# A hybrid convolution and RWKV-7 block: the last LayerNorm split between two phases, and a new fit of the clock that orders the trace

## The chip, the cores and the metric

The kernel runs on one core of one Trainium2 chip. The core has a matrix engine (TensorE, in the profile PE for matmuls and PEld for weight loads), a vector engine (DVE), a scalar engine (ACT), a general engine (POOL) and an engine that here only issues DMAs (SP). Each works through its own queue in order; semaphores join them. The metric is the device time of one execution in microseconds, the median of several runs.

## The reference

One decoder block with two token mixers over 2048 tokens of 1024 channels, all in float32:

```python
h = _rmsnorm(x, norm_g[l]) * (1.0 + scale[:, None, :]) + shift[:, None, :]
p = jnp.einsum('bsd,de->bse', h, w_in[l])
...
u = val * jax.nn.sigmoid(gate)
u = _causal_depthwise_conv(u, conv_k, conv_b)
u = _layernorm(u, ln_g, ln_b, LN_EPS)
u = jax.nn.silu(u) * jax.nn.silu(og)
y_conv = u @ w_o
...
o = _rwkv7_scan(r, decay, k, v, kk, kk * a)
o = _layernorm(o, gn_g, gn_b, GN_EPS)
o = (o + jnp.sum(r * k * r_k, axis=-1, keepdims=True) * v) * jax.nn.silu(og)
y_rwkv = o @ w_o
...
m = jax.nn.sigmoid(g_conv) * y_conv + jax.nn.sigmoid(g_rwkv) * y_rwkv
x = x + gate[:, None, :] * jnp.einsum('bsd,de->bse', m, w_out[l])
return _rmsnorm(x, final_g)
```

The LayerNorm of this study is the one over the 1024 channels of the convolution's output `u`, separately for each token.

## The kernel before

**Tiling.** The 2048 tokens are four blocks of TB = 512 (NB = 4). A tile is 128 channels by 512 tokens, so a block's convolution output is eight tiles (KT = 8). Each float32 matmul against a weight is three matmuls: the operand and the weight are each split into a rounded high part and the rest (`h_hi`, `h_lo`, `w_hi`, `w_lo`), and high-high, high-low and low-high are summed. One projection of 128 output channels is 8 x 3 = 24 matmuls of 512 columns.

**Two phases.** The first phase goes through the blocks b = 0 to 3. For each it projects 73 tiles of the input projection, runs the convolution's taps on DVE (`taps`: one multiplication and 30 multiply-adds a tile), and works the RWKV state in four groups g of four heads, in chunks of 64 tokens. Its results go to scratch in HBM: `z_d` (RWKV branch, gated), `y_d` (convolution output), `co_d` (its gate), `u_d` (convolution branch after LayerNorm and gates), `gr_d` and `gc_d`. At its end `rows0` does the two branch projections of block 0 ("ro" and "co"). The second phase does what is left, block by block: output projection with the residual (`pout`, `addx`), final RMSNorm (`tail_rs`, `finish`, store to `out`), and the branch projections of the next block (`rproj`, `cproj`). It loads z and u tiles (`lsplit`, through 8 load buffers `ld`) and splits them again. A finished x tile and the branch sum `mr` of the next block share one buffer, so `mr` waits for the store of `out`.

**The order of the first phase.** It is written out by a planner that runs while the kernel is traced. Tasks are Python generators with a rank; each `yield` gives a time from which the task may go on. `note` (line 89) keeps a model clock for each engine: an operation's time is a constant plus a slope times the elements per partition, by `RATE`, and for a DMA issue a constant on SP. PE's model time `now` moves with the projections, and between them `poll` lets each task go on whose time has come. So the modelled durations do not change an operation, but they set where it stands in its engine's queue, and so what a matmul behind it waits for. `Load.steps` also uses the clocks: the low part of a weight is made on POOL, or on DVE when POOL's clock is later than DVE's by more than 0.3 us (W2). Input weights are split in block 0 alone and kept in HBM (`kh_in`, `kl_in`). The second phase is ordered by the framework's own scheduler, from program order.

**Slots.** One slot is one group of one block: 6 projections for two pairs of heads (k, r, v each), and filler projections between them, given by FILL or, for the last block, by LAST ("c" is a convolution tile, "1" to "4" are gates). `order` puts FIRST fillers behind the first pair and the rest behind the second. `pair` makes the matrices of two heads (tiles KR, BK, As, tk, uv), `group` solves the triangular systems (a loop of POOL operations on `itmp` and `TT`, then small matmuls through `Tn` and `Qs`), runs the chain over 8 chunks (`S`, `Se`, `xo`), normalises and writes z. `slot` waits at its start until the group two before is normalised.

**Side work.** `sides` runs beside the slots: the next block's RMSNorm, the LayerNorm of the block before (`lnorm_first`), and `presplit`, which splits and stores weights of the second phase ahead of time. All draw their buffers from one ring `hx` of 7 tiles. The LayerNorm has three passes over the eight tiles: a sum (mean), centred squares with the centred tiles stored again (variance), and the last pass, which multiplies by the reciprocal root, applies the gain, bias, tanh and gate, and stores u. Each pass loads the tiles from HBM. For the last block `last_norm` runs all three, with its additions on DVE, once the last convolution tile is there; it has its own ring `more`, to which `lend(3)` gives three tiles of `hx`. The first operand of `rows0` (z of block 0) is loaded by `hload` from four items before the end of the last slot on.

Of the kernel before, what the change touches and what calls it, by code (L numbers as in the profile page):

```python
# [45 lines left out]
SLACK = 2.0  # L46
KEPT = ("in",)
# [4 lines left out]
FIRST = 5  # L52
AHEAD = 0.7
# [21 lines left out]
def hybrid_block(ctx: ExitStack, tc: tile.TileContext, x, vecs, convk, w2a2, final_g, ada, w_in, w_co, w_ro, w_o, crow, out,  # L75
# [12 lines left out]
    def note(name, op, out, ins):  # L88
        k_ = key(out)
        t = max([now[0], vt.get(name, 0.0), used.get(k_, 0.0) if name != "PE" or k_[:2] != "xo" else 0.0] + [ready.get(key(a), 0.0) + SEM for a in ins])  # L90
        if k_ not in ready and getattr(out.tensor, "tag", None):
            past, n = tags.setdefault(out.tensor.tag, []), out.tensor.tag_meta.bufs
            free_ = sorted((max(ready.get(q, 0.0), used.get(q, 0.0)) for q in past), reverse=True)
            if len(free_) >= n:
                t = max(t, free_[n - 1])
            past.append(k_)
            del past[:-3 * n]
        if name == "PE":
            if op == "transpose":
# [12 lines left out]
        elif name == "SP":  # L112
            vt["SP"] = t + 0.36
            vt["DMA"] = max(vt["DMA"], t) + size(out) * out.shape[0] * 4 / DMA_RATE
            end = vt["DMA"] + 1.9
        else:
            c0, c1_ = RATE[name] if op != "memset" else (0.1, 0.9e-3)
            end = vt[name] = t + c0 + c1_ * max([size(out)] + [size(a) for a in ins[:1]])
        ready[k_] = max(ready.get(k_, 0.0), end)
        for a in ins:  # L120
            used[key(a)] = max(used.get(key(a), 0.0), end)
# [154 lines left out]
    u_dram = scratch("u_d")  # L276

# [245 lines left out]
    hx = Ring(HXB, hx0)  # L523
    t2r = Ring(T2B, lambda name: e2.tile([P, TB], F32, name=name, tag="t2", bufs=T2B))
# [252 lines left out]
    def pair(G, q_, box):  # L777
        b, pr, uv, Asb = G.b, 2 * G.g + q_, G.uv, G.As[q_]
# [37 lines left out]
        yield ok(k)  # L816
        KR = l3.tile([P, NCH // 2, 4 * CH], F32, name="KR", tag="KR", bufs=KRB)
# [75 lines left out]
        yield when(lambda: "v" in box)  # L893
# [26 lines left out]
    def group(G, before):  # L920
        g, b, As, uv, R = G.g, G.b, G.As, G.uv, G.R
# [51 lines left out]
        yield when(lambda: G.pairs == 2 and (before is None or before.chained))  # L973
        yield ok(*As)
# [79 lines left out]
        locked[0] = False  # L1054
# [135 lines left out]
    convs = []  # L1190

    def taps(b, j, u, before):
# [18 lines left out]
    def lnorm_first(b, hx):  # L1211
# [9 lines left out]
        yield hx.room(3, 1)  # L1221
        ys, nxt = yload(0), yload(1)
        for j in range(1, KT):
            yj = nxt
            if j + 1 < KT:
                yield hx.room(1, 1)
                nxt = yload(j + 1)
            yield ok(ys, yj)
            eng.tensor_tensor(out=ys, in0=ys, in1=yj, op=ALU.add)
            hx.give(yj)  # L1230
# [34 lines left out]
        hx.give(qs, rt, mean)  # L1265
        def both_of(j):
            yj, ct = yload(j), hx.take("lnc")
            nc.sync.dma_start(ct, co_dram[b][j])
            return yj, ct

        nxt = None
        for j in range(KT):
            if nxt is None:
                yield hx.room(3, 1)
                nxt = both_of(j)
            else:
                yield hx.room(1)
            yj, ct = nxt
            th, nxt = hx.take("lnth"), None
            if j + 1 < KT and b + 1 == NB and hx.room(2)() is not None:  # L1280
                nxt = both_of(j + 1)
# [80 lines left out]
    def sides(b, g):  # L1362
# [51 lines left out]
    def order(b, g):  # L1414
# [31 lines left out]
    def slot(b, g, h, lora, new):  # L1446
        until(lambda: not Gs[:-1] or Gs[-2].normed)
# [129 lines left out]

    def cproj(b, uhl, mhl):
# [41 lines left out]
    for b in range(NB):  # L1620
# [73 lines left out]
        if b + 1 < NB:  # L1694
            uhl = lsplit(u_dram[b + 1], utiles())
# [40 lines left out]
```

## Time and profile before

| | |
|---|---|
| median of 3 runs | 2889.28 us |
| lowest and highest | 2885.52 and 2889.45 us |
| profiled execution, device time | 2893.26 us |
| its span, first to last instruction | 2891.5 us |
| granted TensorE clock, mean | 0.984 |
| ACT and POOL busy | 38% and 41% of the span |

The span is what the profile can explain; the device time of the same execution is 1.8 us longer. A group of instructions is named out<-in by the program's tiles. All first-phase instructions are recorded through one helper, so their line is that of the helper (L132) and the tile names tell them apart. A matmul's busy time includes part of its pipeline, so busy PE is not PE at its peak.

### The profile page before, as it was taken

Reading aid. Unit: us, or ns where it says so; the run is one execution under the profiler, and the core shown is the slowest. Engines: PE = TensorE matmul, PEld = TensorE weight load, DVE = VectorE, ACT = ScalarE, POOL = GpSimd, SP = SyncE. Lnnn points to the kernel's source line nnn. Section 1 sums busy time; section 2 is a strip of 40 time slices with the busy share of each in tenths; the row PEclk is TensorE's granted clock in tenths of the full one; section 3 lists DMA queues with packets and bytes.
Section 4 is the critical chain, followed back from the end, with each engine's and each line's share of the span. In section 5 each row is a group of like instructions: output and inputs, shape, how many; then the busy total and the mean of one; then the engine's idle time right before and its main releaser. Section 6 shows DMA issues by size and latency. Waiting matters only on the chain. (4 is left out here: it accounts for less than half of the span.)

```text
span 2891.5 us, 52406 instructions
## 1 busy us (share of the span) xinstructions
PE 2722.4 (94%) x19472; PEld 2195.2 (76%) x19472; DVE 2067.5 (72%) x3598; ACT 1092.9 (38%) x2181; POOL 1195.6 (41%) x1725
## 2 busy tenths in 40 slices
PE   6999999989999999999999998999999998999998
PEld 5777777767777777777777776877777777898988
DVE  6877887869677878886878786888887576343343
ACT  5545444434243434443434343324343334121211
POOL 1564746533528364534564553474543612000000
PEclk9999999989999999999999999999999999999999
DMA  8776867666758677767666776676665778777664
GB/s 329 258 286 206 292 218 265 236 233 228 235 185 290 199 255 242 275 222 238 231 251 223 249 255 197 220 269 215 227 230 191 273 247 315 259 239 247 215 226 175
DMA packets 370959, 697.26 MB, mean 241 GB/s; under 512 B 135184, under 2 KB 153936, under 8 KB 370704
## 3 DMA queue, kind: packets, MB, share of 16 engines
q1 hardware_dynamic: 370704, 693.91, 70.3%
q8 instruction: 154, 2.52, 0.4%
q14 instruction: 101, 0.83, 0.1%
HBM read 500.63 MB, written 192.02 MB: 240 GB/s over the span
## 5 line engine op out<-in xcount | busy, mean ns | idle before, releaser
L132 PE MATMUL ps_main<-h_hi,w_hi 128*128 128x512 f32 x2432 | 1016.3, 418 | 16.7 <-DVE lora L132 4.6
L132 PE MATMUL ps_main<-h_hi,w_lo 128*128 128x512 f32 x2432 | 966.9, 398 | 25.3 <-POOL w_lo L132 14.6
L132 PE MATMUL ps_main<-h_lo,w_hi 128*128 128x512 f32 x2432 | 961.3, 395 | 0.5 <-DVE h_lo L132 0.5
L132 DVE SCALAR_TENSOR_TENSOR acc<-u,ck,acc 128x512 f32<-128x512 f32 x928 | 698.0, 752 | 27.9 <-POOL u L132 2.2
L132 PEld LDWEIGHTS ps_main<-h_hi,w_lo 128*128 128x128 f32 x2432 | 462.2, 190 | 140.1 <-POOL w_lo L132 18.7
L132 PEld LDWEIGHTS ps_main<-h_hi,w_hi 128*128 128x128 f32 x2432 | 463.3, 190 | 128.4 <-issue 13.3
L132 PEld LDWEIGHTS ps_main<-h_lo,w_hi 128*128 128x128 f32 x2432 | 463.7, 191 | 96.3 <-issue 8.7
L132 POOL TENSOR_TENSOR w_lo<-w_st,w_hi 128x1024 fp32r<-128x1024 f32 (+1 forms) x82 | 165.0, 2012 | 332.5 <-ACT w_hi L132 288.5
L132 ACT ACTIVATE th<-ps_main 128x512 f32<-128x512 f32 x160 | 95.5, 597 | 360.2 <-PE ps_main L132 311.5
L132 POOL TENSOR_TENSOR TT<-TT,itmp 128x126 f32<-128x126 f32 (+22 forms) x496 | 209.5, 422 | 38.9
L132 POOL TENSOR_TENSOR itmp<-La,TT 128x126 f32<-128x126 f32 (+22 forms) x496 | 203.5, 410 | 37.7 <-issue 7.9
L132 ACT CAST w_hi<-w_st 128x1024 fp32r<-128x1024 f32 (+1 forms) x135 | 127.4, 945 | 221.6 <-DMA w_st<-w_co_t 78.4
L132 DVE SCALAR_TENSOR_TENSOR S<-xo,pe,Se 64x64 f32<-64x64 f32 x512 | 145.0, 283 | 91.9 <-PE xo L132 69.4
L132 ACT COPY uv<-xo 64x256 f32<-64x256 f32 (+1 forms) x192 | 81.2, 439 | 251.3 <-PE xo L132 184.7
L132 DVE TENSOR_TENSOR w_lo<-w_st,w_hi 128x1024 fp32r<-128x1024 f32 x53 | 74.5, 1405 | 68.3 <-PE ps_main L132 51.6
L132 DVE TENSOR_TENSOR As<-aux,maskA 128x512 f32<-128x512 f32 x128 | 82.3, 685 | 49.0 <-PE aux L132 48.9
L132 ACT ACTIVATE Se<-S,pe 128x128 f32<-128x128 f32 x256 | 89.0, 397 | 67.2 <-DVE S L132 66.7
L132 PEld LDWEIGHTS aux<-KR,BK 64*128 64x128 f32 x1024 | 66.3, 191 | 44.3 <-POOL KR L132 21.1
L132 PE MATMUL aux<-KR,BK 64*128 64x128 f32 x1024 | 80.0, 290 | 20.7 <-POOL KR L132 14.0
L132 POOL TENSOR_TENSOR wlo<-wf,wl 64x128 fp32r<-64x128 f32 x64 | 31.3, 489 | 159.2 <-ACT wl L132 156.7
L132 DVE TENSOR_TENSOR xt<-pout,xt 128x256 f32<-128x256 f32 x64 | 24.4, 420 | 100.1 <-PE pout L132 100.1
L132 PEld LDWEIGHTS xo<-S,KR 128*128 128x128 f32 x512 | 77.1, 189 | 20.7 <-ACT Se L132 4.3
(283 smaller groups left out, 5005.4 us busy)
## 6 DMA issues: line engine op xcount, KB each, us to landing
w_hi<-kh_in SPq DMA_DIRECT2D x219, 512.0 KB
w_lo<-kl_in SPq DMA_DIRECT2D x219, 512.0 KB
w_st<-w_in_t SPq DMA_DIRECT2D x73, 512.0 KB
kh_in<-w_hi SPq DMA_DIRECT2D x71, 512.0 KB
kl_in<-w_lo SPq DMA_DIRECT2D x71, 512.0 KB
lny<-y_d SPq DMA_DIRECT2D x96, 256.0 KB
w_hi<-kh_ro SPq DMA_DIRECT2D x32, 512.0 KB
w_lo<-kl_ro SPq DMA_DIRECT2D x32, 512.0 KB
```

What stands on the lines that cost most here:

```text
L132: r = f(*a, **k)
```

## The change

**The last LayerNorm.** For the last block, `taps` copies the first finished convolution tile to a sum tile and adds each later one to it. `lnorm_first` then starts with the sum that is given to it and leaves out the first pass. After the reciprocal roots it stores them (`rl_d`) and ends; the last pass of the last block is done by `ulast` in the second phase, ahead of the last `cproj`, from `y_d`, `co_d` and `rl_d`, and its result is split at once, without going through `u_d`. For the other blocks the last pass keeps its form, without a branch for loading the next pair of tiles early, which only the last block took. `lend` gives one tile, not three.

**The clock.** A DMA issue takes 0.45 us of SP's clock, not 0.36; an ACT operation takes 0.1 us more for each operand beyond the first; the scan's slope is doubled; a DVE multiply-add of 64 elements takes 0.08 us more.

**The slots.** A slot no longer waits for the group two before. Instead `pair` allocates its As tile once that group's chain has ended, and the uv tile is allocated when that group is normalised; `group` loads its matrices (`La`) once the group before has merged its own. In the last slot one filler stands behind the first pair instead of five (FIRST_LAST), and the loads of z start 9 items before the end instead of 4 (HLAST). The 16 pre-splits are spread over blocks 1 to 3 as 1, 1, 2, 2 and 1, 1, 2, 2 and 1, 1, 1, 1 a slot (LATE_W), instead of 1, 1, 3, 3 in blocks 1 and 2.

```diff
+LEND = 1
+LATE_W = ((), (1, 1, 2, 2), (1, 1, 2, 2), (1, 1, 1, 1))
+FIRST_LAST = 1
+HLAST = 9
...
         elif name == "SP":
-            vt["SP"] = t + 0.36
+            vt["SP"] = t + 0.45
...
             c0, c1_ = RATE[name] if op != "memset" else (0.1, 0.9e-3)
-            end = vt[name] = t + c0 + c1_ * max([size(out)] + [size(a) for a in ins[:1]])
+            n_ = max([size(out)] + [size(a) for a in ins[:1]])
+            if name == "ACT":
+                c0 += 0.1 * max(len(ins) - 1, 0)
+            elif op == "tensor_tensor_scan":
+                c1_ *= 2
+            elif name == "DVE" and op == "scalar_tensor_tensor" and n_ == CH:
+                c0 += 0.08
+            end = vt[name] = t + c0 + c1_ * n_
...
     def pair(G, q_, box):
...
+        yield when(lambda: G.prior is None or G.prior.chained)
+        Asb = l3.tile([P, 2, NCH, P], F32, name="As", tag="As", bufs=ASB)
+        G.As.append(Asb)
...
-        yield when(lambda: "v" in box)
+        yield when(lambda: "v" in box and (G.prior is None or G.prior.normed))
+        if q_ == 0:
+            G.uv = l3.tile([P, NCH, 2, P], F32, name="uv", tag="uv", bufs=2)
...
     def opened(b, g, h, lora):
...
-        G.uv = l3.tile([P, NCH, 2, P], F32, name="uv", tag="uv", bufs=2)
+        G.merged = False
+        G.prior, G.uv, G.As = Gs[-2] if len(Gs) > 1 else None, None, []
-        G.As = [l3.tile([P, 2, NCH, P], F32, name="As", tag="As", bufs=ASB) for _ in range(2)]
...
     def group(G, before):
...
+        yield when(lambda: before is None or before.merged)
         La = lt.tile([P, 32, 32], F32, name="La", tag="La", bufs=1)
...
     def taps(b, j, u, before):
...
+        if b + 1 == NB and j == 0:
+            yield hx.room(1)
+            ysum.append(hx.take("ysum"))
+            nc.scalar.copy(ysum[0], yj)
+        elif b + 1 == NB:
+            yield ok(ysum[0], yj)
+            nc.vector.tensor_tensor(out=ysum[0], in0=ysum[0], in1=yj, op=ALU.add)
...
-    def lnorm_first(b, hx):
+    def lnorm_first(b, hx, ys=None):
...
+        if b + 1 == NB:
+            yield ok(rl)
+            nc.sync.dma_start(rl_d, rl)
+            hx.give(rl)
+            return
...
     def sides(b, g):
...
-                yield from lend(3)
+                yield from lend(LEND)
         if b:
-            for _ in range(0 if b + 1 == NB else (1, 1, 3, 3)[g]):
+            for _ in range(LATE_W[b][g]):
...
-        yield from lnorm_first(NB - 1, more)
+        yield from lnorm_first(NB - 1, more, ysum[0])
...
-            yield from fill(FIRST if q == 0 else len(todo))
+            yield from fill(len(todo) if q else FIRST_LAST if (b, g) == (NB - 1, 3) else FIRST)
...
     def slot(b, g, h, lora, new):
-        until(lambda: not Gs[:-1] or Gs[-2].normed)
...
-            if new is not None and rest == 4:
+            if new is not None and rest == (4 if b + 1 < NB else HLAST):
...
+    def ulast(hl):
+        rl = f2.tile([P, TB], F32, name="rl", tag="rl", bufs=1)
+        nc.sync.dma_start(rl, rl_d)
+        for j in range(KT):
+            yt, ct = ldt("yt", y_dram[NB - 1][j]), ldt("ct", co_dram[NB - 1][j])
+            th = ob.tile([P, TB], F32, name="uth", tag="uth")
+            nc.vector.tensor_tensor(out=yt, in0=yt, in1=rl, op=ALU.mult)
+            nc.scalar.activation(th, yt, AF.Tanh, scale=hlg[:, j:j + 1], bias=hlb[:, j:j + 1])
+            nc.scalar.activation(yt, yt, AF.Identity, scale=vc("conv_ln_g", j), bias=vc("conv_ln_b", j))
+            nc.vector.scalar_tensor_tensor(out=yt, in0=th, scalar=1.0, in1=yt, op0=ALU.add, op1=ALU.mult)
+            nc.vector.tensor_tensor(out=yt, in0=yt, in1=ct, op=ALU.mult)
+            split(hl[0][j], hl[1][j], yt, nc.vector)
+        return hl
...
-            uhl = lsplit(u_dram[b + 1], utiles())
+            uhl = lsplit(u_dram[b + 1], utiles()) if b + 2 < NB else ulast(utiles())
```

More of the change, by code (lines that the diff above doesn't have):

```diff
@@ L276, in hybrid_block @@
     u_dram = scratch("u_d")
+    rl_d = dp.tile([P, TB], F32, name="rl_d", tag="rl_d")
     grow_d = dp.tile([D], F32, name="grow_d", tag="grow_d")
@@ L523, in hybrid_block @@
     hx = Ring(HXB, hx0)
+    hx1 = hx
     t2r = Ring(T2B, lambda name: e2.tile([P, TB], F32, name=name, tag="t2", bufs=T2B))
@@ L777, in pair @@
     def pair(G, q_, box):
-        b, pr, uv, Asb = G.b, 2 * G.g + q_, G.uv, G.As[q_]
+        b, pr = G.b, 2 * G.g + q_
         wf = e1.tile([P, 2, P], F32, name="wf", tag="wf")
@@ L892, in pair @@
         nc.scalar.copy(rk, pb)
-        yield when(lambda: "v" in box)
+        yield when(lambda: "v" in box and (G.prior is None or G.prior.normed))
+        if q_ == 0:
+            G.uv = l3.tile([P, NCH, 2, P], F32, name="uv", tag="uv", bufs=2)
+        uv = G.uv
         vv = box["v"]
@@ L920, in group @@
     def group(G, before):
-        g, b, As, uv, R = G.g, G.b, G.As, G.uv, G.R
+        g, b, As, R = G.g, G.b, G.As, G.R
         yield when(lambda: G.tri == 2)
@@ L973, in group @@
         yield when(lambda: G.pairs == 2 and (before is None or before.chained))
+        uv = G.uv
         yield ok(*As)
@@ L1053, in group @@
                     cp(As[q][prow(e), :, e::2, rcol(e)], pg[e].rearrange("p c (h n) -> p h c n", h=2)[prow(e ^ q)])
-        locked[0] = False
+        locked[0], G.merged = False, True
         O = uv[:, 0::2]
@@ L1188, in conv @@
         evac(value(project(h, ("in", T_VAL + j)), convs[-3:-2]))
-    convs = []
+    convs, ysum = [], []
     def taps(b, j, u, before):
@@ L1220, in lnorm_first @@
         eng = nc.vector if b + 1 == NB else nc.gpsimd
[L1221 to L1230, printed above, removed]
+        if ys is None:
+            yield hx.room(3, 1)
+            ys, nxt = yload(0), yload(1)
+            for j in range(1, KT):
+                yj = nxt
+                if j + 1 < KT:
+                    yield hx.room(1, 1)
+                    nxt = yload(j + 1)
+                yield ok(ys, yj)
+                eng.tensor_tensor(out=ys, in0=ys, in1=yj, op=ALU.add)
+                hx.give(yj)
         yield burst(ok(ys), free, bank("late"))
@@ L1264, in lnorm_first @@
                 yield idle("DVE", 0.3)
-        hx.give(qs, rt, mean)
-        def both_of(j):
-            yj, ct = yload(j), hx.take("lnc")
-            nc.sync.dma_start(ct, co_dram[b][j])
[L1269 to L1281, printed above, removed]
+        hx.give(qs, rt)
+        hx1.give(mean)
+        if b + 1 == NB:
[4 more added lines that the diff above has]
+        for j in range(KT):
+            yield hx.room(3, 1)
+            yj, ct, th = yload(j), hx.take("lnc"), hx.take("lnth")
+            nc.sync.dma_start(ct, co_dram[b][j])
             yield ok(yj, rl)
@@ L1576, in lsplit @@
         return hi, lo
+    def ulast(hl):
+        rl = f2.tile([P, TB], F32, name="rl", tag="rl", bufs=1)
+        nc.sync.dma_start(rl, rl_d)
+        for j in range(KT):
+            yt, ct = ldt("yt", y_dram[NB - 1][j]), ldt("ct", co_dram[NB - 1][j])
[7 more added lines that the diff above has]
+        return hl
     def cproj(b, uhl, mhl):
```

## The prediction

> **What bounds the kernel now.** I read the page first: the span, the busy shares and the slices.
>
> ```profile
> span 2891.5 us, 52406 instructions
> PE 2722.4 (94%) x19472; PEld 2195.2 (76%) x19472; DVE 2067.5 (72%) x3598; ACT 1092.9 (38%) x2181; POOL 1195.6 (41%) x1725
> ...
> PE   6999999989999999999999998999999998999998
> ...
> DVE  6877887869677878886878786888887576343343
> ```
>
> TensorE is the bound. It is busy for 2722 of 2891.5 us, its work is the same matmuls after the change, and so a change can only win the 169 us in which it stands idle, and what a lowered clock adds to them. VectorE is next: seven to eight tenths through the first phase, three to four tenths in the last fifth. So I asked second where the idle time lies, stage by stage (columns: stretch, length, busy time and count of PE, PEld, DVE, ACT, POOL, granted clock, DMA share, GB/s).
>
> ```profile
> core 0: us, PE busy (x) PEld busy (x) DVE busy (x) ACT busy (x) POOL busy (x), PEclk, DMA share, GB/s
> ...
> 2300.00:2310.00 10.00, 6.98 (x25) 5.13 (x24) 3.79 (x6) 4.26 (x7) 8.04 (x19) 0.84 0.88 341
> ...
> 2360.00:2410.00 50.00, 44.86 (x244) 35.75 (x243) 46.35 (x70) 24.52 (x39) 22.58 (x10) 1.00 0.64 212
> ...
> 2420.00:2440.00 20.00, 12.63 (x99) 11.55 (x98) 12.43 (x22) 10.86 (x24) 0.00 (x0) 0.91 1.02 373
> ...
> 2702.00:2748.00 46.00, 46.00 (x389) 45.84 (x388) 12.61 (x27) 11.99 (x38) 0.00 (x0) 1.00 0.57 202
> ...
> 570.00:600.00 30.00, 19.43 (x63) 14.28 (x63) 25.53 (x34) 5.81 (x9) 25.73 (x53) 0.78 0.85 314
> ```
>
> The reader is to see three kinds of stretch. From 2300 to 2440, where the first phase hands over to the second, PE idles 3.0, 5.1 and 7.4 us in the three quoted pieces. In the second phase (2702 to 2748) it is never idle, and DVE has 33 of 46 us free. In the first phase there are stretches such as 570 to 600, with 10.6 us idle. A lowered clock comes with the worst of them: 0.78 of 30 us is 6.6 us more, 0.84 of 10 us is 1.6, 0.91 of 20 us is 1.8.
>
> Third, the chain of waits over the handover.
>
> ```profile
> 2398.93 4.60 DVE lny L132 x2
> ...
> 2405.12 1.04 ACT w_hi L132
> 2406.24 2.67 POOL w_lo L132
> ...
> 2420.74 5.32 DMA zt<-z_d
> 2426.07 6.92 DMA xt<-x_in
> 2433.05 7.24 DMA w_lo<-kl_o
> ```
>
> Here the last pass of the last LayerNorm (tile lny) stands directly ahead of a weight split that PE needs, and then three loads follow one another: the second phase's first tiles are fetched only when the first phase lets go, and the weights of the output projection queue behind them.
>
> **The last pass, moved.** Part by part, beginning with what leaves the first phase.
>
> ```profile
> L132 DVE SCALAR_TENSOR_TENSOR lny<-lnth,lny 128x512 f32<-128x512 f32 x8 | 9.4, 1173 | 0.6 <-ACT lny L132 0.4
> ...
> L132 DVE TENSOR_TENSOR lny<-lny,lnr 128x512 f32<-128x512 f32 x7 | 8.1, 1153 | 0.1
> L132 DVE TENSOR_TENSOR lny<-lny,lnc 128x512 f32<-128x512 f32 x8 | 7.6, 954 | 0.0
> ...
> L132 ACT ACTIVATE lnth<-lny,hlb,hlg 128x512 f32<-128x512 f32 x8 | 6.5, 811 | 9.7 <-DVE lny L132 9.7
> ```
>
> These rows are of 2343 to 2416 alone. Three DVE operations for each of 8 tiles, 25 us, and two ACT operations of about 0.81 us each, 13 us, leave the stretch in which DVE is at 46.35 of 50 us. With them go 24 transfers (y and conv gate in, u out), and one small store of the reciprocal roots comes in. PE's 5.1 us of idle in 2360 to 2410 is not all theirs: the group chain and the load of the next operand tiles stay. I take half, **-2.6 us**; ends 0 and -5.1.
>
> In the second phase the same operations come back as ulast, with two loads per tile instead of one. There POOL does nothing, and the nearest row, the split of the same tile, gives the price of one two-input operation.
>
> ```profile
> L132 DVE TENSOR_TENSOR u_lo<-zt,u_hi 128x512 fp32r<-128x512 f32 x24 | 15.3, 687 | 7.4 <-ACT u_hi L132 7.4
> ```
>
> 24 operations of 0.69 us are 16.5 us of DVE, and 16 of 0.81 us are 13.0 us of ACT. They lie beside the third block's output projection, whose 46 us (2702 to 2748) have 33.4 us of DVE and 34.0 us of ACT free: hidden. One tile worked alone is 4 DVE and 3 ACT operations, 4 x 0.69 + 2 x 0.81 + 0.6, about 5 us; eight in strict sequence would be 40 us, still inside. If that cover failed, what waits is the end of the block, which has no slack:
>
> ```profile
> 2753.53 4.11 DMA out<-xt
> ...
> 2757.77 0.70 DVE mr L132
> 2758.51 76.46 PE ps_main L132 x336
> ```
>
> PE starts on the result of `mr` at once, and `mr` needs a tile freed by the output store. Every microsecond by which ulast keeps DVE past 2748 is paid. Behind ulast's loads, which wait for one of 8 load buffers, SyncE's queue holds the weight loads of the next projections; they are loaded two pairs ahead, more than one tile's 5 us. I put **+1.5 us**, ends -0.5 and +6.
>
> **The sum, moved.** The first pass was 7 DVE additions and 8 loads after the last convolution tile. Now it is one ACT copy and the same 7 additions, each behind its tile, and no loads. Work on DVE is unchanged, and the mean is there as soon as the eighth tile is. Second pass and roots stay. Cost nothing: the additions ride with the taps, which have the lowest rank, and the last convolution (c7) stands in the third of the last block's four groups; without that cover it would be 7 x 0.9 = 6 us of DVE at the handover. The price is the row of the additions:
>
> ```profile
> L132 DVE TENSOR_TENSOR lny<-lny 128x512 f32<-128x512 f32 x15 | 12.8, 856 | 11.7 <-DMA lny<-y_d 11.6
> ```
>
> **The last group and the operand loads.** HLAST starts the loads of the first phase-two operand 9 items before the end, no longer 4. Between 2300 and 2440 the waits of PE say who lacked them:
>
> ```profile
> PE ps_main L132 <- ACT h_hi L132: 2.8, 1, 2.8
> ```
>
> This is the 3.0 us idle of 2300 to 2310, and the 1.6 us of clock with it: **-4.4 us**; ends 0 and -4.6. [...] The quoted stretch shows 0.84 with a longest wait of 2.8 us, so the measurement decides and the clock stays in.
>
> FIRST_LAST puts the last pair of heads behind one filler projection, not five. Its triangular solve and its chain now end inside the tail:
>
> ```profile
> L132 POOL TENSOR_TENSOR itmp<-La,TT x31: 239/410/892, 2273.6 to 2308.6; 128x126 f32<-128x126 f32 x3, 128x30 f32<-128x30 f32 x2, 128x56 f32<-128x56 f32 x2, 128x78 f32<-128x78 f32 x2
> ...
> L132 DVE STREAM_TRANSPOSE Tn<-As x8: 392/433/443, 2323.0 to 2329.4; 32x256 f32<-32x256 f32 x8
> ```
>
> Four projections less ahead of it are at least 22 us (24 matmuls each, at 76.46 / 336 = 0.23 us by the chain row above), so the chain starts near 2300 or before, and the stretch after 2380 holds little but projections. Together with the vanished last pass, whose tiles hold space up to the end of its stretch, 2416, the 8 x loads and 8 z loads can go out before the last projection ends instead of at 2420, and the weights behind them come sooner. What PE loses there is 7.4 us idle and 1.8 us of clock. I take two thirds, **-6.1 us**; ends 0 (the operand tiles of the last projection hold the space, not the LayerNorm) and -9.2.
>
> **The order of the first phase.** The clock that orders the trace now charges 0.45 us for a DMA issue, 0.1 us per extra ACT operand, a doubled slope for the scan (0.15 + 512 x 0.0022 = 1.28 us, from 0.71) and 0.08 us more for the state update (0.30 from 0.22). It changes no operation, only where each stands in its queue. The rows that it was held against:
>
> ```profile
> L132 DVE SCALAR_TENSOR_TENSOR S<-xo,pe,Se 64x64 f32<-64x64 f32 x512 | 145.0, 283 | 91.9 <-PE xo L132 69.4 <-ACT Se L132 5.7 <-issue 1.8
> ...
> L132 DVE TENSOR_TENSOR_SCAN M<-keep,M 128x512 f32<-128x512 f32 x32 | 44.4, 1388 | 8.4 <-ACT M L132 8.1
> ```
>
> ```profile
> 2420.26 1.37 SPq L132 DMA_DIRECT2D zt<-z_d  x3
> ```
>
> 283 ns, 1388 ns, and 1.37 / 3 = 0.46 us for an issue: each new charge is nearer than the old one. So matmuls are placed later where they used to be placed ahead of their inputs. What that can win are PE's waits between 60 and 2295 us for ACT and DVE:
>
> ```profile
> PE aux L132 <- ACT sq L132: 12.9, 13, 3.2
> PE ps_main L132 <- POOL w_lo L132: 12.8, 6, 4.6
> PE late L132 <- DVE Tn L132: 11.3, 7, 3.3
> PE aux L132 <- DVE As L132: 6.3, 8, 2.7
> ...
> PE aux L132 <- ACT tk L132: 4.0, 10, 1.5
> PE xo L132 <- DVE uv L132: 3.7, 7, 1.0
> ```
>
> Without the POOL row they are 38.2 us. One operation's charge is only part of what makes an input late, and a new order makes waits of its own, so I take a quarter, **-10 us**; ends -38 (all of them) and +17 (one more stretch like 570 to 600, 10.6 idle and 6.6 of clock). The other waits that the change adds (for the earlier group's chain, normalisation or merge, in place of one wait for all at the start of a slot) hold back the placing of instructions, no engine; I count them here, with the four weight pre-splits that move from blocks 1 and 2 into block 3, whose results are first read after 2440.
>
> **Sum.** -2.6 + 1.5 - 4.4 - 6.1 - 10 = -21.6 us against the profiled execution's 2893.3 us, or 2871.7. That execution is 4.0 us above the median of the runs shown, 2889.3; from there it is **2868 us**.
>
> **Rivals.** *The tail has another wall.* If space for the second phase is let go by the last projection itself, the handover stays: -15.5 us, 2874. For it: the x loads follow the end of the last projection at once. Against: w_lo comes last of all, behind 16 loads that need not wait for it. 12 in 100. *The fit does more.* If half of the 38.2 us goes and half of 570 to 600's loss with it, the order term is -28, and with the whole handover, 9.2, the time is 2847. 14 in 100. *No change.* The order term turns to +11, as waits of new places replace those of old ones, and the tail's gain is spent: 2889. 12 in 100. *Slower, by the choice of engine for the weight splits.* The planner gives a split to DVE when POOL's clock is more than 0.3 us behind.
>
> ```profile
> L132 POOL TENSOR_TENSOR w_lo<-w_st,w_hi 128x1024 fp32r<-128x1024 f32 (+1 forms) x82 | 165.0, 2012 | 332.5 <-ACT w_hi L132 288.5
> ...
> L132 DVE TENSOR_TENSOR w_lo<-w_st,w_hi 128x1024 fp32r<-128x1024 f32 x53 | 74.5, 1405 | 68.3 <-PE ps_main L132 51.6
> ```
>
> The new fit makes DVE's clock later, by 2 x 0.57 + 32 x 0.08 = 3.7 us a group, and leaves POOL's, so more splits go to POOL, at 2.0 us instead of 1.4. In block 0, where each input tile is split once, POOL is busy 25.73 of 30 us in 570 to 600, and PE waits there for w_lo. A second stretch of that kind, 17.2 us, and the other half of the 12.8 us doubled, 6.5, make +23.7 in place of -10: 2889.3 - 11.6 + 23.7 = 2901. It decides from the point where the order term passes +17.4. Against: DVE at 25.53 of 30 us there has no more room than POOL. 15 in 100.
>
> **Chances.** My forecast 47, and with it the other wall 12 and the stronger fit 14: faster 73 in 100; no change 12; slower 15. A difference of 0.2%, 5.8 us, is about what a measurement of this kernel can tell from none. The range 2846 to 2894 leaves out half of the stronger fit and some two thirds of the slower case.
>
> **What would show it.** Right: PE's wait for h_hi near 2300 is gone; no lny operation after about 2340, and u's operations on DVE between two output stages late in the run with PE still busy throughout; the idle time at the handover under 4 us; PE's waits for sq and Tn smaller. Wrong: a PE gap where the fourth block starts (ulast not hidden), waits for POOL's w_lo above 13 us in the first block, or a handover that still idles 7 us.

## The result, and the profile after

The changed kernel takes **2863.03 us** (median of 4 runs, 2856.74 to 2867.68), the kernel before 2887.60 us beside it (4 runs): a ratio of 0.9909, interval 0.9887 to 0.9931. The profiled execution took 2867.68 us, its span 2866.0 us, against 2893.26 and 2891.5 us: 25.6 us less. The median lies 5 us under the forecast of 2868 us and inside its range. Several of the forecast's terms were nevertheless far off, and their errors cancel, as the experiments show.

The page of the changed kernel, the lines that stand for those shown of before (the span, PE's busy time, and PE and DVE in 40 slices):

```profile
span 2866.0 us, 52384 instructions
PE 2712.4 (95%) x19472; PEld 2198.5 (77%) x19472; DVE 2056.0 (72%) x3596; ACT 1091.8 (38%) x2182; POOL 1194.2 (42%) x1727
...
PE   6999999989899999999999999999999998998998
...
DVE  6877787868677787886778787898887564335343
```

PE runs the same 19472 matmuls. So the 25.5 us of span are idle time, or the lengthening that goes with it. To see where, I cut both traces at places with the same work behind them. The table by stretches, first of the kernel before, then of the changed one (columns as in the prediction):

```profile
60.00:2300.00 2240.00, 2128.29 (x15755) 1678.44 (x15754) 1746.21 (x2991) 911.95 (x1810) 1155.29 (x1682) 0.99 0.70 238
...
60.00:2428.00 2368.00, 2245.01 (x16670) 1772.01 (x16669) 1845.20 (x3150) 961.36 (x1894) 1192.01 (x1715) 0.99 0.71 239
2428.00:2880.00 452.00, 439.43 (x2629) 391.82 (x2628) 170.47 (x308) 96.68 (x219) 0.00 (x0) 0.99 0.70 240
```

```profile
60.00:2270.00 2210.00, 2117.62 (x15770) 1681.14 (x15768) 1738.96 (x2990) 909.46 (x1808) 1148.79 (x1693) 0.99 0.71 239
...
60.00:2391.00 2331.00, 2230.83 (x16670) 1771.89 (x16669) 1817.72 (x3122) 947.91 (x1878) 1190.60 (x1717) 0.99 0.71 239
2391.00:2860.00 469.00, 444.31 (x2637) 395.92 (x2635) 191.91 (x362) 109.69 (x239) 0.00 (x0) 0.97 0.69 238
```

The first 15,755 matmuls took 2240 us, and 15,770 now take 2210: **30 us** less. The whole first phase and the handover, 16,670 matmuls each time, went from 2368 to 2331 us: **37 us**, of which the tail of the first phase has 7. The second phase gave some back: from these cuts to the end of the span it is 463.5 us before and 475.0 us now. That is **+12 us**, and the idle time in the rows doubled from 12.6 to 24.7 us. The three make -25. Of the first 37, 23 are idle time (123.0 to 100.2 us). The other 14 are busy time of the same number of matmuls. The records of matmuls overlap (those of pout at 2690 us in the changed kernel start 0.12 us apart and last 0.28 us each). The sum of busy time fell with no matmul less, and what the 14 us are made of stays open.

What the first phase's waits became (waits of PE between 60 and 2295 us in the changed kernel; total us, times, longest):

```profile
PE aux L143 <- POOL KR L143: 20.4, 11, 6.7
PE ps_main L143 <- POOL w_lo L143: 12.9, 7, 3.3
PE late L143 <- DVE Tn L143: 8.1, 6, 2.5
...
PE aux L143 <- ACT tk L143: 6.1, 10, 1.5
...
PE aux L143 <- ACT sq L143: 3.4, 7, 0.8
...
PE aux L143 <- DVE As L143: 2.2, 3, 0.9
...
PE xo L143 <- DVE uv L143: 1.3, 4, 0.4
```

The waits for sq, Tn, As and uv that the prediction had named fell from 34.2 to 15.0 us; tk, which it had named too, rose from 4.0 to 6.1, and w_lo stayed. One is new in size, KR with 6.7 us at its longest. Its cause stands in the trace of POOL, row by row (start, duration, then in brackets the idle time before it and what ended it):

```profile
775.99 1.26 POOL L143 TENSOR_TENSOR w_lo<-w_st,w_hi 128x512 fp32r<-128x512 f32 x1 [5.61 <-ACT w_hi L143]
777.21 1.17 POOL L143 TENSOR_TENSOR KR<-r,E 128x512 f32<-128x512 f32 x1
```

Half of a weight split (128x512 is the shape of the pre-splits, which aren't needed before the second phase) stands in front of KR in POOL's queue and waits 5.6 us for w_hi, and PE waits for the KR behind it.

The handover still idles. The chain of waits there, and the stretch's row:

```profile
2377.92 5.28 PE ps_main L143 x23
2383.20 0.10 SPq L143
...
2383.87 6.59 DMA zt<-z_d
```

```profile
2383.00:2403.00 20.00, 12.34 (x99) 11.33 (x97) 12.94 (x22) 9.50 (x22) 0.00 (x0) 0.93 1.00 358
```

Idle are 7.7 us of 20, against 7.4 before. The first of the loads goes out within 0.2 us of the end of the last projection (2383.20), and the last thing that the last LayerNorm does is to store its roots, some 80 us sooner:

```profile
L143 SPq DMA_DIRECT2D rl_d<-lnr x1: 319/319/319, 2300.8 to 2300.8; - x1
```

So it isn't the LayerNorm that held their space.

In the second phase the loss is one gap. The stretch at the start of the third block:

```profile
2578.00:2602.00 24.00, 14.04 (x55) 10.99 (x55) 21.55 (x46) 10.80 (x18) 0.00 (x0) 0.79 0.95 346
```

PE is idle for 10.0 of 24 us, at a clock of 0.79. Something of ulast is in the way there, though ulast is written behind the *third* block's output projection. DVE started it a block early, at the end of the *second* (operations on ulast's tile yt: count, shortest, median and longest ns, first and last start):

```profile
L143 DVE TENSOR_TENSOR yt<-yt,rl x8: 684/691/693, 2577.4 to 2611.6; 128x512 f32<-128x512 f32 x8
```

What it does there is seen on DVE's own rows, in order of time:

```profile
2582.27 0.17 DVE L143 TENSOR_REDUCE vs<-sq 128x4 f32<-128x16 f32 x1
2582.39 0.69 DVE L143 TENSOR_TENSOR yt<-yt,ct 128x512 f32<-128x512 f32 x1
2583.00 0.16 DVE L143 TENSOR_SCALAR vs<-vs 128x4 f32<-128x4 f32 x1
2583.07 0.68 DVE L143 SCALAR_TENSOR_TENSOR yt<-uth,yt 128x512 f32<-128x512 f32 x1
...
2590.63 0.69 DVE L143 TENSOR_TENSOR yt<-yt,rl 128x512 f32<-128x512 f32 x1 [1.33 <-DMA yt<-y_d]
2591.24 0.16 DVE L143 SCALAR_TENSOR_TENSOR rs<-rs_t,rs 128x4 f32<-128x4 f32 x1
2591.43 5.39 DVE L143 SCALAR_TENSOR_TENSOR xt<-xt,rs,fg 128x512 f32<-128x512 f32 x8
```

The block's reciprocal roots (vs, rs, rs_t) are twelve operations of 0.16 us, each of which needs the one before. Between them stand operations of ulast of 0.69 us, and one of these waits 1.33 us for its load. From the first small operation (2582.27) to the scaling of xt (2591.43) go 9.2 us, and `mr`, on which PE waits, comes behind that.

### The profile page after: what moved, and what is told of

The parts are those of the page before. It is cut to its first block, busy times and chain, and to the rows that moved or that the text cites. A ratio compares the mean times of both kernels' runs of the same rounds, so it can differ in the third digit from the quotient of the medians.

```text
span 2866.0 us, 52384 instructions
## 1 busy us (share of the span) xinstructions
PE 2712.4 (95%) x19472; PEld 2198.5 (77%) x19472; DVE 2056.0 (72%) x3596; ACT 1091.8 (38%) x2182; POOL 1194.2 (42%) x1727
## 5 line engine op out<-in xcount | busy, mean ns | idle before, releaser
L143 PE MATMUL ps_main<-h_hi,w_lo 128*128 128x512 f32 x2432 | 967.7, 398 | 22.9 <-POOL w_lo L143 12.9
L143 ACT ACTIVATE t<-ps_main,mu 128x512 f32<-128x512 f32 x96 | 65.9, 687 | 85.7 <-PE ps_main L143 77.0
```

What stands on the lines that cost most here:

```text
L143: r = f(*a, **k)
```

## The experiments

The theory after this reading: the order of the first phase won 30 us, by the fit and the freed slots together; moving the last pass won something in the tail and cost 12 us in the second phase; the handover won nothing. The main rivals: the order is chance (another order, another time), one of the two parts does it alone, or the tail won it. All times are medians, all ratios against the kernel before, run beside each; 0.001 of ratio is 2.9 us.

| kernel | median, us (runs) | ratio | interval |
|---|---|---|---|
| changed kernel | 2863.03 (4) | 0.9909 | 0.9887 to 0.9931 |
| e1_hold | 2850.56 (4) | 0.9867 | 0.9842 to 0.9891 |
| e2_oldclock | 2889.90 (10) | 1.0009 | 0.9991 to 1.0026 |
| e3_onlyclock | 2911.00 (4) | 1.0086 | 1.0063 to 1.0108 |
| e4_sp044 | 2869.57 (4) | 0.9937 | 0.9917 to 0.9957 |
| e5_gate | 2891.51 (10) | 1.0016 | 0.9990 to 1.0042 |
| e6_tail | 2878.92 (10) | 0.9967 | 0.9948 to 0.9985 |
| e7_latew | 2868.97 (10) | 0.9930 | 0.9911 to 0.9949 |
| e8_gate_oldclock | 2902.80 (10) | 1.0046 | 1.0028 to 1.0065 |
| e9_nolast | 2878.26 (7) | 0.9955 | 0.9939 to 0.9971 |
| e10_handover | 2854.64 (6) | 0.9873 | 0.9847 to 0.9900 |
| e11_nolast_oldtail | 2890.63 (12) | 1.0015 | 1.0000 to 1.0030 |
| e12_nolast_early | 2865.94 (6) | 0.9923 | 0.9897 to 0.9950 |

**e1_hold: ulast kept behind the second block's end.** No operation of ulast may stand on DVE ahead of the last scaling of the second block.

```diff
-            uhl = lsplit(u_dram[b + 1], utiles()) if b + 2 < NB else ulast(utiles())
+            if b + 2 < NB:
+                uhl = lsplit(u_dram[b + 1], utiles())
+            else:
+                with tc.issue_after(held_[0]):
+                    uhl = ulast(utiles())
```

> The changed kernel with one edge more: the operations of the moved last pass (ulast) may not stand ahead of the last finish operation of the second block on their engine. Theory: ulast was let in at the end of the second block's output projection, where its vector operations stand between the small steps of finish and one of them waits 1.3 us for a load; that is the 10.0 us gap and the lowered clock behind it, and without it the gap falls to the 2.5 us of before, the time to about 2851 us. Rival: the gap is the transfer queue's, full at that place (0.95 of its engines), so the loads that stay there keep it: 2860 us or more, gap above 7 us.

Measured: 2850.56 us, 12.5 under the changed kernel. The same stretch in its trace:

```profile
2578.00:2602.00 24.00, 21.79 (x95) 17.50 (x94) 20.40 (x41) 9.03 (x12) 0.00 (x0) 1.00 0.98 362
```

PE's idle time in it is 2.2 us, not 10.0, and the clock is full. The roots now stand by themselves, 2.4 us from the first to the scaling:

```profile
2577.64 0.16 DVE L143 TENSOR_REDUCE vs<-sq 128x4 f32<-128x16 f32 x1
...
2580.02 5.39 DVE L143 SCALAR_TENSOR_TENSOR xt<-xt,rs,fg 128x512 f32<-128x512 f32 x8
```

The loss was 7.8 us of idle time and the lowered clock behind it, and it is gone. The clock cost less than (1 - 0.79) x 24 = 5.0 us: most of the stretch at half clock, 2591.4 to 2598.6 us (0.50), lies in the gap itself, where PE has nothing to run, and only 3.1 us of it lie behind, some 1.5 us lost. From its cut at 2391 us to the end of the span e1_hold takes 463.3 us, the changed kernel 475.0, the kernel before (from 2428) 463.5: kept in its place, ulast costs the second phase nothing. The theory stands, and this is the fastest median of all the kernels here.

**e2_oldclock and e3_onlyclock: the fit, taken away and alone.** e2 is the changed kernel with the old four charges; e3 is the kernel before with the new ones.

```diff
-            n_ = max([size(out)] + [size(a) for a in ins[:1]])
...
-            end = vt[name] = t + c0 + c1_ * n_
+            end = vt[name] = t + c0 + c1_ * max([size(out)] + [size(a) for a in ins[:1]])
...
-            vt["SP"] = t + 0.45
+            vt["SP"] = t + 0.36
```

> The changed kernel with the four old charges of the ordering clock. Theory: the new fit is what shortens the first phase by some 31 us up to its last slot, so without it the time goes back to about 2880 to 2890 us. Rival: the freed slots (no wait for the group two before) and the moved side work do it, and the time stays at 2858 to 2870 us.

> The kernel before with the four new charges alone. Theory of the fit: 2860 to 2870 us, since it lacks the gap of the second phase but also the freed slots. Rival (slots and side work): 2880 to 2895 us. PE's wait for sq, 12.9 us before, falls to about 4 us if that wait is the charges' work.

Measured: 2889.90 and 2911.00 us. Given the rest of the change the fit wins 27 us, as the theory for e2 said; without the rest it loses 0.0086, some 25 us, slower than both the theory and the rival for e3. The waits of PE for sq in the two (60 to 2295 us):

```profile
PE aux L136 <- ACT sq L136: 13.8, 13, 3.2
```

```profile
PE aux L139 <- POOL KR L139: 16.9, 10, 6.7
...
PE ps_main L139 <- DMA w_hi<-kh_in: 7.6, 3, 4.1
...
PE aux L139 <- ACT sq L139: 4.8, 6, 1.7
```

So the fit does what it was fitted for: sq falls from 12.9 to 4.8 us even alone, and the long KR wait is its price in either kernel (in e2 the longest is 1.9 us). But alone it opens other waits, among them 4.1 us for the weights of one projection, of which the kernel before had 0.6 at most. By 2300 us the two come out level: e3 has 15,750 matmuls behind it since 60 us, the kernel before 15,755. Most of the 25 us are lost later, in the last slot and at the handover, where PE's longest wait for xt is 9.1 us against 3.5. The four charges were changed together in all runs, so which of them does it is open.

**e4_sp044: how much is chance.** One charge changed by a hundredth, from 0.45 to 0.44 us, which no theory gives a meaning.

```diff
-            vt["SP"] = t + 0.45
+            vt["SP"] = t + 0.44
```

> A control: the changed kernel with 0.44 instead of 0.45 us for a DMA issue, which reorders a little and changes no reason. It shows how far the time moves by a new order alone. If the gain is the fit's, the time stays within 6 us of 2863; if any new order is worth 10 us either way, no part of the change that shifts less than that can be told from chance.

Measured: 2869.57 us, 6.5 more. One arbitrary new order is worth 6.5 us, and I take that as the size of chance: nothing smaller can be put down to a part. It is one control only. The 27 of the fit are four times that.

**e5_gate and e8_gate_oldclock: the slots.** e5 makes a slot wait again for the group two before; e8 does so with the old charges as well.

```diff
+        until(lambda: not Gs[:-1] or Gs[-2].normed)
         G = opened(b, g, h, lora)
```

> The changed kernel with the wait at the start of a slot back (the group two before must be normalised). Theory: the new charges make normalisation later on the ordering clock, and a slot that waits for it lets PE's place in the order stand still, so the fit only pays where slots are free: 2880 us or more, with gaps of 3 to 5 us ahead of projections at slot starts, as in the run of the charges alone. Rival: the loss of that run comes from its old LayerNorm and pre-splits, and the time stays within 7 us of 2863.

> The changed kernel with both the slot's wait and the four old charges back: the fourth corner beside the changed kernel (2863), old charges with free slots (2890) and new charges with the wait. Theory: with old charges the wait hardly binds, so 2885 to 2895 us, near the 2890 of free slots. Rival: free slots are worth 10 us or more by themselves, then 2900 or more.

Measured: 2891.51 and 2902.80 us: for e5 the theory stands (its longest wait for the weights of a projection, w_hi, is 4.3 us), for e8 the rival. With e2 and the changed kernel this is a table of four:

| | slots free | slots wait |
|---|---|---|
| new charges | 2863.0 | 2891.5 |
| old charges | 2889.9 | 2902.8 |

The freed slots win 28.5 us with the new charges and 12.9 with the old ones; the fit wins 26.9 with free slots and 11.3 with waiting ones. Either gain is smaller by 15.6 us without the other. Four cells stand in that difference, each with a chance of its own; at 6.5 us a cell chance alone could make some 13, so the interaction isn't shown by the times. Freed slots also win without the fit, 12.9 us or twice what the control moved: likely a worth of their own, but from one order each.

The traces show the gain in the first phase itself. Between 60 and 2270 us the nine kernels with both parts (the changed one, e1, e4, e6, e7 and e9 to e12) run 15,753 to 15,786 matmuls; with freed slots alone (e2) it is 15,666, with the fit alone (e5, e3) 15,660 and 15,625, with neither (e8, the kernel before) 15,607 and 15,634. Several of the nine have an order of their own, so the 30 us are not one lucky order; and added to e8 the two single gains would make 15,719, fewer than any of the nine. Why e3 loses where e5 against e8 gains isn't settled: they differ in everything else that was changed, and no run here splits it further.

**e6_tail: the tail's two constants.**

```diff
-FIRST_LAST = 1
-HLAST = 9
+FIRST_LAST = 5
+HLAST = 4
```

> The changed kernel with FIRST_LAST = 5 and HLAST = 4. Theory: the early loads and the early last pair are worth 4 to 7 us, so 2867 to 2870, with a wait of about 3 us for h_hi at the start of the branch projections. Rival: the last pair's place alone moves work from one stretch of full PE to another, and the time stays within 3 us of 2863.

Measured: 2878.92 us, 16 more than the changed kernel, more than twice what was expected. The expected wait for h_hi isn't there: between 2160 and 2440 us the list of PE's waits has none for h_hi, but 3.8 us for another tile of ACT (th). What the profile shows is less than 16 us. PE's waits in the tail, 2375 to 2425 us:

```profile
PE pout L143 <- DVE xt L143: 6.8, 1, 6.8
...
PE late L143 <- POOL uv L143: 2.6, 1, 2.6
```

The last group's chain (uv) now ends in the handover, and the wait for xt is 6.8 us. Its profiled execution, 2872.27 us, is only 4.6 us above that of the changed kernel and lies at the low end of its runs, so the rest of the 16 us isn't in this trace.

**e7_latew: the old places of the pre-splits.**

```diff
-LATE_W = ((), (1, 1, 2, 2), (1, 1, 2, 2), (1, 1, 1, 1))
+LATE_W = ((), (1, 1, 3, 3), (1, 1, 3, 3), (0, 0, 0, 0))
```

> The changed kernel with the pre-splits at their old places (1, 1, 3, 3 in blocks 1 and 2, none in block 3). Theory: POOL and the ring of seven tiles are what holds block 2 and block 1 back, and the time goes up by 5 to 15 us. Rival: pre-splits are hidden wherever they stand; the time moves by no more than the control did, 7 us.

Measured: 2868.97 us, 5.9 more, no more than e4 moved by chance. Undecided.

**e9_nolast, e11_nolast_oldtail and e12_nolast_early: the last pass back in the first phase.** e9 undoes the move (the running sum stays), e11 sets FIRST_LAST and HLAST back too, and e12 gives e9 the early loads that the code before had.

```diff
-        if b + 1 == NB:
-            yield ok(rl)
-            nc.sync.dma_start(rl_d, rl)
-            hx.give(rl)
-            return
...
-            uhl = lsplit(u_dram[b + 1], utiles()) if b + 2 < NB else ulast(utiles())
+            uhl = lsplit(u_dram[b + 1], utiles())
```

> The changed kernel with the second half of the moved last pass undone: normalisation, tanh and gate of the last LayerNorm are worked and stored in the first phase again (behind the same last convolution), and the second phase loads the finished u as before; the running sum, FIRST_LAST, HLAST, the freed slots and the fit stay. Theory (the last pass costs the second phase some 12 us at its third block, as e1_hold found, and the tail some 3 us where it stood before): about 2853 us, with the idle time ahead of the third block back at 2 to 3 us. Rival (the last pass had to leave the first phase for the shorter tail to work, as its 25 us of DVE and 24 transfers stand ahead of the last operand splits): above 2860 us, and PE's idle time between 2250 and 2400 larger by 5 us or more.

> e9_nolast with FIRST_LAST and HLAST at their old values 5 and 4 as well: of the change stay the running sum, the freed slots, the fit and the places of the pre-splits. Theory (the moved last pass and the new tail pay only together: in e9_nolast the last pass stands alone behind the last projection, one tile in 7 us, since nothing is left to cover it; with four projections back behind the last heads it is covered again): faster than e9_nolast, about 2872 us, and PE idle 10 us or less between the last projection and the second phase's first one, against 23 there. Rival (the last pass is late by its own chain behind the last convolution, whatever the tail): 2878 us or more, and 20 us idle or more still.

> e9_nolast with the early loads of the code before restored in the last pass: the next tile's two transfers go out while the current one is worked, where buffers are free. FIRST_LAST and HLAST keep their new values. Theory (most of what e9_nolast lost is the loop's one tile at a time: 97 us for 8 tiles there, 79 us before): the last pass ends some 15 us sooner, PE idles under 10 us ahead of the second phase's first projection, and the time is about 2863 us. Rival (the pass stands behind the last group's work in DVE's order and is the wall of the tail wherever its loads are): 2874 us or more, with 15 us idle or more.

Measured: 2878.26, 2890.63 and 2865.94 us. My theory for e9 (about 2853) fell. PE's longest wait in its handover, and the first operation of each tile in the last pass (first and last start behind the durations):

```profile
PE pout L143 <- ACT o_hi L143: 23.1, 1, 23.1
```

```profile
L143 DVE TENSOR_TENSOR lny<-lny,lnr x8: 672/692/1381, 2317.8 to 2411.1; 128x512 f32<-128x512 f32 x8
```

The eight tiles are begun over 93 us, one behind the other, and PE idles 23.1 us until they are done. For e11 I had thought that the old tail would cover them again; it idles 20.5 us, so that fell too, and both rivals stand. e12 shows how much was the loop: with the early loads the wait for o_hi is 16.3 us and the time 2865.94 us, within 3 us of the theory, though the idle time is the rival's. The tiles are now begun from 2310.4 to 2391.3 us. PE's wait, and pieces of the chain of waits that leads to it:

```profile
PE pout L143 <- ACT o_hi L143: 16.3, 1, 16.3
```

```profile
2394.47 0.70 DVE lny L143
...
2395.55 6.59 DMA zt<-z_d
...
2402.19 0.62 ACT o_hi L143
```

The load of the second phase goes out behind the last tile of the pass, and the operand's split behind the load. So with the pass in the first phase, the handover waits for it. Against the changed kernel the difference is 0.0014 of ratio, inside the intervals, because the pass in the second phase costs 12.5 us there. Against e1_hold, where it costs next to nothing, it is 0.0056, **16 us**. That is what the move is worth against e12. The pass there is not quite the old one: its ring still has one lent tile (LEND), the code before lent three, and no run tries three.

**e10_handover: the order on DVE at the handover.** e1_hold, with the next block's z splits held behind the first residual additions, and the x tiles loaded first halves first.

```diff
-        if b + 1 < NB:
+        if b and b + 1 < NB:
             ohl = lsplit(z_dram[b + 1], okt(b + 1))
...
+            if b == 0:
+                with tc.issue_after(held_[0]):
+                    ohl = lsplit(z_dram[1], okt(1))
```

> e1_hold with two things changed at the handover alone: the split of the next block's z tiles is issued behind the residual additions of the first column block, not ahead of them, and the x tiles are loaded first halves first. Theory (the handover idles because DVE, in order, stands at the z splits, which wait for their loads, while PE waits for the additions to free its accumulators): PE's idle time from 2383 to 2403 falls from about 7 to about 3 us, and the time is about 2845 us, 5 under e1_hold. Rival (the wall is the space that the last projection lets go and the full transfer queue behind it, 358 GB/s in that stretch): the same time as e1_hold within 3 us, 2848 to 2854, and about 7 us idle still.

Measured: 2854.64 us. The stretch from 2383 us, first in e1_hold, then in e10:

```profile
2383.00:2403.00 20.00, 12.85 (x101) 12.25 (x102) 12.32 (x22) 9.40 (x22) 0.00 (x0) 0.93 1.01 377
```

```profile
2383.00:2403.00 20.00, 18.62 (x149) 17.68 (x147) 9.39 (x17) 6.57 (x16) 1.43 (x2) 1.00 1.02 374
```

The two rows don't begin at the same work: the last projection ended at 2382.5 us in e1_hold and at 2386.0 us in e10, so 3 us of the second row are still projection. Counted from that end, PE idles 7.4 us of the first 20 in e1_hold and 3.0 in e10, as the theory wanted; of the next 20 it idles none and 1.8. The clock of these 40 us is 0.91 and 1.00. From the end of the last projection to that of the span e10 takes 3.8 us less, but the first phase, which the edit doesn't touch, took 3.5 us more in this execution. The theory's 2845 us did not come: the ratio is 0.9873 against 0.9867, the same within the intervals. The rival is right on the time, the theory on the wait. Whether a gain of a few us is there, these runs can't tell.

## Why the prediction came out right, and where it was wrong

**The order of the first phase: -10 predicted, -30 measured.** The mechanism was right and the size was not, though it is inside its ends of -38 and +17. Of the 38.2 us of named waits 17.1 went, and other waits, KR above all, rose; in the rows at equal work the 30 us are 19.3 us of idle time and 10.7 us of busy time, of which the -10 had no share. The step that failed is "so I take a quarter" of 38.2 us of named waits, and beside it the half sentence that the freed slots "hold back the placing of instructions, no engine; I count them here". Putting the wait back (e5) costs 28.5 us, putting the charges back (e2) 26.9: the freed slots are as large a part as the fit, and I had no separate price for them. The fit alone (e3) is 25 us slower than the kernel before, so "each new charge is nearer than the old one" was no argument for a gain by itself.

**The last pass leaving the first phase: -2.6 predicted, about -16 measured** (e12 against e1_hold). The step was "I take half" of 5.1 us of idle time. That priced the pass by the idle time beside it in the trace of before, where nothing else was ready sooner. Once the rest came 30 us forward, the pass came only 20 (its last store of u starts at 2395.2 us in e12, at 2415.3 before), and was the end of the phase: in e12 PE waits 16.3 us for the operand tiles behind it.

**ulast in the second phase: +1.5 predicted, +12.5 measured** (e1). The rule of the prediction, that DVE held past the end of a block is paid, was right, and the place was wrong: "They lie beside the third block's output projection". The instructions were started one block sooner, between the small operations at the end of the second block, and made 9.2 us of 2.4. The sign that I had named, a gap where the fourth block starts, isn't there:

```profile
2723.00:2733.00 10.00, 9.95 (x44) 7.89 (x42) 8.04 (x22) 0.62 (x4) 0.00 (x0) 1.00 0.75 244
```

**The operand loads (HLAST): -4.4 predicted, not shown as theirs.** The wait for h_hi is shorter, and the clock stays at 1.00 around it (2268 to 2278 us). But e6, with HLAST at 4 again, has no such wait either, so these runs don't show that the early loads did it. And a wait that the profile gives no releaser for ("issue") stands some 34 us later. Waits of PE between 2262 and 2350 us, and the stretch that holds the one without a releaser:

```profile
PE ps_main L143 <- issue: 2.7, 1, 2.7
...
PE ps_main L143 <- ACT h_hi L143: 1.4, 1, 1.4
```

```profile
2300.00:2310.00 10.00, 7.28 (x151) 5.74 (x143) 4.03 (x7) 2.13 (x4) 0.00 (x0) 0.83 0.89 317
```

It begins at 2302 us, within another projection and right behind 128 small matmuls. The operand isn't what it waits for: the last of its eight low halves (h_lo) was ready at 2273 us. Its cause stays open.

**The handover: -6.1 predicted, none.** The idle time is 7.7 us, over the 4 us that the prediction gave as a sign and past the 7 that it called wrong. The step was that the x and z loads "can go out before the last projection ends". They go out from 0.2 us after it, so the rival of the other wall was right in its mechanism: by the chain, space is let go by the last projection, not by the LayerNorm. Taken together the two constants are worth up to 16 us (e6), against 10.5 predicted for them and the last pass's space. The trace of e6 shows one way, the last group's chain in the handover, for a part of it.

**The slower rival** needed more weight splits on POOL. There are 84 instead of 82, and PE's wait for them is 12.9 us, 12.8 before. It didn't happen. Its price of 17.2 us for a stretch like 570 to 600 was also 1.7 too high: between 578.4 and 583.0 us PE is idle at a clock of 0.64, and the sum counts that time twice.

**The sum.** Predicted: -10 for the order, -13.1 for the tail with the last pass, +1.5 for ulast. The traces have -30, -7 and +12. The tail's own -7 doesn't contradict the 16 us of the move: what the tail parts did was mostly to let the 30 us through. e11 has neither the move nor the new constants (nor the early loads of the code before, worth 9 to 12 us by e12 against e9):

```profile
60.00:2270.00 2210.00, 2115.88 (x15753) 1679.91 (x15752) 1743.20 (x2993) 911.51 (x1810) 1145.30 (x1668) 0.98 0.72 240
...
60.00:2428.00 2368.00, 2237.01 (x16661) 1776.16 (x16660) 1838.72 (x3151) 963.25 (x1898) 1198.64 (x1718) 0.98 0.71 239
```

It has as many matmuls behind it at 2270 us as the kernel before at 2300, and no more than that one at 2428: the 30 us were won and lost again in the tail. That the forecast came within 5 us is luck: a gain put 20 us too low met two results put 6 and 11 us too well.

## What to carry to other kernels

Price a part that is moved off the end of a phase by what it would hold up if everything else came sooner, not by the idle time beside it today. Where a compiler's scheduler may move work, its place in the code proves nothing: read in the trace where it runs, and hold it there if it would come between the small steps that the next stage waits for. Try a fit of a model clock with its gates freed as well as without, and measure the worth of one arbitrary new order before believing any part that is smaller than that.

## What the runs showed of the hardware

The granted clock was lowered behind short stops of PE, but their length alone doesn't decide. In the changed kernel the longest wait between 2300 and 2310 us is 2.7 us, and the granted clock of those 10 us is 0.83 (the row above); between 734 and 745 us the clock is 0.84 with no wait above 1.3 us. In the kernel before, a stop of 2.5 us leaves the clock at 1.00 (the idle time of this row is one wait):

```profile
2612.00:2626.00 14.00, 11.51 (x50) 9.01 (x49) 10.81 (x27) 1.67 (x6) 0.00 (x0) 1.00 1.03 362
```

In e10, whose longest waits at the handover are these, it stays at 1.00 too:

```profile
PE pout L143 <- DMA w_hi<-kh_o: 1.9, 2, 1.6
PE pout L143 <- DMA w_lo<-kl_o: 1.5, 2, 0.8
```

What decides beside the length, no run here separates. What stood behind other work in an engine's queue was held up with it, as the traces show twice. On POOL, KR stood behind a split that waited 5.6 us for w_hi, and PE waited 6.7 us for KR. On DVE, the small operations of the second block's end stood among those of ulast, one of which waited 1.33 us for its load, and with ulast held behind them the time is 12.5 us less (e1_hold).
